# RWKV-7 and neighbourhood-attention trunk on one core: the inputs of the second and third stream of products are split one stream earlier

## The chip, the core and the metric

One core of a Trainium2 chip runs the whole program in one launch. The metric is the device time of one execution in microseconds (us). TensorE (PE) multiplies matrices, VectorE (DVE) and ScalarE (ACT) work on elements, GpSimd (POOL) sets small tiles and issues part of the stores, and SyncE (SP) issues the other DMAs. PSUM holds the results of products.

## What is computed

Two request groups of 512 tokens by 1024 features go through two layers with shared weights. Layer 0 is RWKV-7 time mixing, scanned forward and backward; layer 1 is 2-D neighbourhood attention. Everything is fp32.

```python
xx = 0.5 * (x_prev + x_next) - xn
lerp = lambda j: xn + xx * mu[j]
r = heads(lerp(0) @ w_r).astype(f32)
k = heads(lerp(1) @ w_k).astype(f32)
v = heads(lerp(2) @ w_v).astype(f32)
z = xn @ w_z
kk = k * k_k.astype(f32).reshape(N_HEADS, HEAD_DIM)
kk = kk / jnp.maximum(jnp.sqrt(jnp.sum(kk * kk, axis=-1, keepdims=True)), 1e-12)
...
for d in range(2):
    ...
    ys.append(_wkv7_scan(r, decay, k_d, v, -kk, kk * a, reverse=(d == 1)))
```

Layer 0 ends with a group norm per head, a gate by z and the product with `w_o`; layer 1 multiplies by `w_in` (1024 x 4096), attends within a window and multiplies by its own output weights.

## The kernel before

Activations lie with features on the 128 partitions and the 512 tokens along them, so a matrix of 1024 features is 8 tiles, called k tiles here. A product of one column (128 output features) takes 8 k tiles. fp32 operands are cut into a high and a low half (`halves`: ACT copies the rounded high half, DVE subtracts it), and a k tile costs three matmuls: high by high, high by low, low by high (L454 to L456 in `gemm`, L887 to L889 in the later stage). A column is therefore 24 matmuls. Its weights come as two raw tiles of 128x512 which are cut in the same way into `whi` and `wlo`, of which there are four buffers each (`NW`). Input halves lie in 18 buffers named `act`.

The program has four stages.

- **The head.** `prelude(0)` loads and normalises the first request group (its 1/rms comes from two small products, L482 and L496, in `rstd`), makes the low-rank products (L595 to L597; their weights lie in 16 buffers `lw`) and mixes neighbouring tokens for v (`mixed`, tiles `ls`, four buffers, stored to scratch DRAM). `prelude(1)` does the same for the second group, and mixes k, r and v for it. Both are generators; `run` takes one step of them for each k tile of PE's columns. PE's columns are first z (8 columns, products in PSUM tiles `zy`), then k (8 columns). The z columns read the unnormalised input (`xz`, 16 of the 18 `act` buffers).
- **Between them** `shifted(0, 1)` mixes k's inputs of the first group (a "lerp": ACT scales, DVE adds, tile `xr`) and cuts them into `act` halves. After the k columns `shifted(0, 0)` does the same for r.
- **The scan stage** (`scan_phase`). A planner (`weave`) interleaves threads by an estimate of when each engine is free, and the order that it finds is fixed for PE, DVE and ACT. `flow` runs the stream of 84 columns (r, v, then the second group's k, low-rank and z, r, v, then the first group's `w_o`, the rest of z, and 24 columns of `w_in`). `preps` makes the scan's factors of a pair of heads, `inverse` and `merges` invert small triangular matrices (DVE's elimination, L1096 and L1098, begins with a transpose at L1089), and `step` runs 64 scan steps, 8 for each of 8 pairs (L1298 is the product that solves a step). Where the planner foresees PE idle for over 0.3 us after a slack stretch it puts in a matmul without use (L1729, "filler"), which the hardware runs as two passes. The tiles of this stage (`k`, `r`, `rb`, `ab`, `cab`) lie where the head's `xn`, `xx`, `ls` and `lw` were, so they wait for these to be read.
- **The rest** is attention and the output products.

In a k column, `column` copies the product (L717), stores it, squares it (L726), sums the squares by head on PE (L730, a product of 2x512), copies the sums (L733) and stores them. After the last column the sums are read back, the square root and reciprocal taken (L744 to L747), stored as `rn`, and read as `rb` by the first `prep` (L962).

Engines take their instructions in order. So do the DMA issuers: an instruction that waits on SP holds up every transfer behind it.

Of the kernel before, what the change touches and what calls it, by code (L numbers as in the profile page):

```python
# [19 lines left out]
P = 128  # L20
T = 512
# [232 lines left out]
class Trunk:  # L254
# [274 lines left out]
    def prelude(self, s):  # L529
        nc = self.nc  # L530
        vt, gps, act = nc.vector, nc.gpsimd, nc.scalar
        xs = []
        if s == 0:
            self.vectors()
        for k in range(KT):
            if s == 0 and k == self.WFIRST:
                self.first = [self.weight(self.a["w_z"][0])]
            t = self.t("xn", (P, T + 2), 16, F32, self.lp)
            self.load(t[:, 1:T + 1], self.a["x"][s][k * P:(k + 1) * P, :])
            xs.append(t)  # L540
# [34 lines left out]
        def mixed(kind, j, k):  # L575

            t = self.t("ls", (P, T), 4, F32, self.lp)
            self.lerp(t, xn[k], xx[k], 8 * j + k)
            self.save("l" + kind, s, k, t)

        if s:
            for k in range(KT):
                for kind, j in (("k", 1), ("r", 0), ("v", 2)):
                    mixed(kind, j, k)
                    yield
                self.save("lz", s, k, xn[k])
            return
        pm = self.p("pf", (P, 2, T))
        ps = (self.p("pm"), self.p("us"))
        for k in range(KT):  # L590
            hi, lo = self.xz[k]
            for q2 in range(2):
                for out, w in ((pm[:, q2], self.wm), (ps[q2], self.wl)):
                    a, b = (m[:, k % 4] for m in w[2 * q2 + k // 4])
                    nc.tensor.matmul(out, a, hi, start=(k == 0), stop=False)  # L595
                    nc.tensor.matmul(out, a, lo, start=False, stop=False)
                    nc.tensor.matmul(out, b, hi, start=False, stop=(k == KT - 1))  # L597
                yield
        for q2 in range(2):
            mw = self.t("lm", (P, T + 2), 1, F32, self.lp)  # L600
            lr = self.t("lr", (P, KT * P), 1, F32, self.lp)
            y, u = lr[:, 0:T], lr[0:64, T:2 * T]
            gps.memset(mw[:, 0:1], 0.0)
            gps.memset(mw[:, T + 1:T + 2], 0.0)
            vt.tensor_tensor(mw[:, 1:T + 1], pm[:, q2], rstd, op=ALU.mult)
            vt.tensor_tensor(y, mw[:, 2:T + 2], mw[:, 0:T], op=ALU.add)
            yield
            vt.scalar_tensor_tensor(mw[:, 1:T + 1], y, 0.5, mw[:, 1:T + 1], op0=ALU.mult, op1=ALU.subtract)
            vt.tensor_tensor(y, ps[q2], rstd, op=ALU.mult)
            vt.tensor_tensor(y, y, mw[:, 1:T + 1], op=ALU.add)  # L610
            for q in (2 * q2, 2 * q2 + 1):
                act.activation(u, y[64 * (q % 2):64 * (q % 2) + 64], AF.Tanh if q < 2 else AF.Copy)
                self.hidden(q, u)
            yield
        for k in range(KT):
            mixed("v", 2, k)
            yield

    def lowrank(self, s, q2, shift, ps):
# [50 lines left out]
        self.nc.scalar.copy(h[0:64], u)  # L670
        self.nc.vector.tensor_tensor(h[64:128], u, h[0:64].bitcast(F32), op=ALU.subtract)

    def lerp(self, t, x, u, i):

        self.nc.scalar.activation(t, x, AF.Identity, scale=self.dv[:, 112 + i:113 + i])
        self.nc.vector.scalar_tensor_tensor(t, u, self.dv[:, 88 + i:89 + i], t, op0=ALU.mult, op1=ALU.add)

    def shifted(self, s, j):
# [93 lines left out]
        self.made.add((kind, s, p))  # L772

    def columns(self, s, kind, x, ps=range(NP)):
        for p in ps:
            w = self.first.pop() if self.first else self.weight(self.a["w_" + kind][p])
            ps = yield from self.gemm(w, x, self.gt)
            for _ in self.column(s, kind, p, ps):
                pass
            yield  # L780

    def flow(self):
# [7 lines left out]
        self.xq, self.post = x, {}  # L790
        for k, t in enumerate(self.groups[0][1]):
            x[0, k] = t

        def loads():
            for c, (_, _, src, _) in enumerate(cols):
                for j in range(2):
                    yield "S", lambda: did["load"] < did["split"] + self.NRAW
                    raw[2 * c + j] = t = self.t("raw", (P, self.WP), self.NRAW)
                    src(t, j) if callable(src) else self.load(t, src[:, j * self.WP:(j + 1) * self.WP])
                    did["load"] += 1  # L800

        def splits():
            for h in range(2 * len(cols)):
# [940 lines left out]
    def scan_phase(self, mid):  # L1744
# [69 lines left out]
        threads = [  # L1814
            Thread(lambda: 0, each(self.step)), Thread(lambda: 0.5, each(self.alone)), Thread(lambda: 0.5, each(self.near)),
            Thread(lambda: 1, each(self.outer)),
            Thread(lambda: 0, fetch()), Thread(lambda: 0, fetch_x()), *self.flow(), Thread(lambda: 5, inverse()), Thread(lambda: 2.4, merges()), Thread(lambda: 1.5, preps()),
            Thread(lambda: 1.3 if did["finish"] == 3 else 4, finish()), Thread(lambda: 1.2, self.norm0(0))]
        e = mybir.EngineType
        with self.tc.manual_schedule(engines={e.PE, e.DVE, e.Activation}):  # L1820
# [3 lines left out]
    def run(self):  # L1824
        self.todo = [(s, pb) for s in range(2) for pb in range(4)]
        self.made, self.hid, self.shift = set(), {}, {}
        self.did = Counter()
        self.xz, self.os = [], [[], []]
        self.spare = None
# [192 lines left out]
```

## Time and profile before

| | before |
|---|---|
| median of 3 runs | 1634.75 us (1633.54 to 1637.68) |
| profiled execution, its own time | 1627.3 us |
| its span from first to last instruction | 1625.5 us |
| PE busy | 1533.3 us, 94% of the span |
| DVE busy | 1218.4 us, 75% |
| ACT busy | 983.7 us, 61% |
| mean granted PE clock | 0.981 |

The profile lists for each engine how long it was busy, for each instruction when it began and what ended the idle time ahead of it, and the clock that PE was granted in a stretch (1.00 is full). Busy times of neighbouring matmuls overlap: a 128x512 matmul shows 0.39 us, but the next begins 0.23 us after it. Of the spans of the stages: the head up to the end of the z columns is 0 to 79.7 us, the k columns and what follows them up to the first r product 79.7 to 153.7, the scan stage 153.7 to about 1137, the rest up to 1625.5.

### The profile page before, as it was taken

The numbers are of one execution on the slowest core, as the hardware profiler recorded it, in microseconds if no ns is written. First come the engines' busy times: TensorE is split into PE (matmuls) and PEld (weight loads), VectorE is DVE, ScalarE is ACT, GpSimd is POOL, SyncE is SP. The second block draws the span as 40 slices with busy tenths as digits, with TensorE's granted clock in tenths as the row PEclk, the third lists the DMA queues.
The fourth block names the chain that finished last, engine by engine and source line by source line (L and its number), as shares of the span: only waits on it lengthen the run. The fifth ranks groups of instructions, "written<-read, shape, count | busy, mean of one in ns | idle before, by whom it ended". The sixth has DMA issues, their size and how long they took to land.

```text
span 1625.5 us, 46341 instructions
## 1 busy us (share of the span) xinstructions
PE 1533.3 (94%) x18748; PEld 1178.7 (73%) x18748; DVE 1218.4 (75%) x2714; ACT 983.7 (61%) x1949; POOL 179.2 (11%) x336
## 2 busy tenths in 40 slices
PE   7989999899989998988999999999999999999998
PEld 6866776666667676766677777777777788777776
DVE  8986587689778787876899998656676575754664
ACT  6567565757648456675666655544667665555562
POOL 0001124201011012231000011000000002100000
PEclk9989999999899999999999999999999999999999
DMA  6447687867576777677776775567664256645553
GB/s 242 158 169 260 212 279 237 270 195 245 167 251 227 239 248 218 224 242 242 247 262 212 233 262 180 160 191 245 196 226 155 93 162 223 224 165 185 163 162 104
DMA packets 182006, 340.46 MB, mean 209 GB/s; under 512 B 25344, under 2 KB 58240, under 8 KB 181792
## 3 DMA queue, kind: packets, MB, share of 16 engines
q1 hardware_dynamic: 158144, 256.75, 49.5%
q0 software_dynamic: 23648, 80.76, 13.9%
q8 instruction: 147, 2.41, 0.6%
q14 instruction: 67, 0.55, 0.1%
HBM read 230.33 MB, written 107.09 MB: 208 GB/s over the span
## 4 chain that ended last, share of the span: by engine, by line
PE 70%; DVE 11%; DMA 7%; issue 5%; ACT 5%; SPq 1%; DVEq 0%; POOL 0%; ACTq 0%; POOLq 0%
PE pm L887 8%; PE pg L454 7%; PE pg L455 6%; PE pg L456 6%; PE pm L888 6%; PE pm L889 6%; PE pf L1199 3%; DMA dab<-ab 2%; PE sc L1537 2%; PE po L1570 2%; PE us L1318 2%; PE pt L1555 2%; PE zy L1271 2%; PE us L1298 2%; DVE ab L1021 1%
## 5 line engine op out<-in xcount | busy, mean ns | idle before, releaser
L887 PE MATMUL pm<-act,whi 128*128 128x512 f32 x672 | 294.6, 438 | 2.7 <-ACT act L832 1.0
L888 PE MATMUL pm<-act,whi 128*128 128x512 f32 x672 | 268.0, 399 | 7.7 <-DVE act L834 6.8
L889 PE MATMUL pm<-act,wlo 128*128 128x512 f32 x672 | 267.3, 398 | 6.6 <-DVE wlo L808 6.6
L887 PEld LDWEIGHTS pm<-act,whi 128*128 128x128 f32 x672 | 127.7, 190 | 45.3 <-issue 12.2
L454 PE MATMUL pg<-act,whi 128*128 128x512 f32 x384 | 160.3, 418 | 0.0
L889 PEld LDWEIGHTS pm<-act,wlo 128*128 128x128 f32 x672 | 128.1, 191 | 37.2 <-DVE wlo L808 8.5
L888 PEld LDWEIGHTS pm<-act,whi 128*128 128x128 f32 x672 | 128.4, 191 | 33.9 <-DVE act L834 11.8
L455 PE MATMUL pg<-act,whi 128*128 128x512 f32 x384 | 152.8, 398 | 0.0
L456 PE MATMUL pg<-act,wlo 128*128 128x512 f32 x384 | 152.3, 397 | 0.0
L404 DVE TENSOR_TENSOR wlo<-raw,whi 128x512 fp32r<-128x512 f32 x148 | 101.6, 689 | 56.1 <-ACT whi L403 55.7
L403 ACT CAST whi<-raw 128x512 fp32r<-128x512 f32 x148 | 91.7, 619 | 83.0 <-PE pg L455 64.9
L808 DVE TENSOR_TENSOR wlo<-raw,whi 128x512 fp32r<-128x512 f32 x168 | 114.6, 684 | 29.1 <-ACT whi L806 29.1
L806 ACT CAST whi<-raw 128x512 fp32r<-128x512 f32 x168 | 103.8, 621 | 45.7 <-PE pm L888 39.5
L456 PEld LDWEIGHTS pg<-act,wlo 128*128 128x128 f32 x384 | 72.2, 188 | 14.9 <-issue 0.3
L454 PEld LDWEIGHTS pg<-act,whi 128*128 128x128 f32 x384 | 72.3, 188 | 14.4 <-issue 3.3
L1098 DVE TENSOR_TENSOR N<-etmp,N 128x30 f32<-128x30 f32 (+14 forms) x240 | 78.9, 329 | 4.6
L455 PEld LDWEIGHTS pg<-act,whi 128*128 128x128 f32 x384 | 72.5, 189 | 13.5 <-issue 2.8
L1096 DVE TENSOR_TENSOR etmp<-N 128x30 f32<-128x30 f32 (+14 forms) x240 | 78.8, 328 | 4.6
L1199 PE MATMUL pf<-cab 64*64 64x128 f32 (+1 forms) x2048 | 68.5, 268 | 6.3 <-issue 5.9
L1551 ACT ACTIVATE sb<-sb,mx 128x256 f32<-128x256 f32 x128 | 64.5, 506 | 11.4 <-DVE mx L1550 10.4
L1548 DVE CUSTOM_DVE_ANT_0 sb<-sc,bias 128x256 f32<-128x256 f32 x128 | 50.1, 420 | 24.3 <-PE pt L1555 13.3
L1310 ACT COPY X<-us 64x256 f32<-64x256 f32 x128 | 47.1, 368 | 33.5 <-PE zy L1177 31.7
(391 smaller groups left out, 3531.3 us busy)
## 6 DMA issues: line engine op xcount, KB each, us to landing
dab<-ab POOLq DMA_DIRECT2D x32, 1024.0 KB, 7.4
cab<-dab SPq DMA_DIRECT2D x64, 512.0 KB
raw<-in_w_in_dram SPq DMA_DIRECT2D x128, 256.0 KB
bias<-in_rpb_dram SPq DMA_DIRECT2D x32, 384.0 KB
raw<-in_w_z_dram SPq DMA_DIRECT2D x32, 256.0 KB
raw<-in_w_k_dram SPq DMA_DIRECT2D x32, 256.0 KB
raw<-in_w_r_dram SPq DMA_DIRECT2D x32, 256.0 KB
k<-dk SPq DMA_DIRECT2D x32, 256.0 KB
```

What stands on the lines that cost most here:

```text
L403: self.nc.scalar.copy(hi, src)
L404: (eng or self.nc.vector).tensor_tensor(lo, src, hi.bitcast(F32), op=ALU.subtract)
L454: nc.tensor.matmul(ps, hi, x[k][0], start=(k == 0), stop=False)
L455: nc.tensor.matmul(ps, hi, x[k][1], start=False, stop=False)
L456: self.mm = nc.tensor.matmul(ps, lo, x[k][0], start=False, stop=(k == KT - 1))
L806: nc.scalar.copy(hi, raw[h])
L808: nc.vector.tensor_tensor(lo, raw.pop(h), hi.bitcast(F32), op=ALU.subtract)
L887: nc.tensor.matmul(ps, hi[:, at], xh, start=(k == 0), stop=False)
L888: nc.tensor.matmul(ps, hi[:, at], xl, start=False, stop=False)
L889: nc.tensor.matmul(ps, lo[:, at], xh, start=False, stop=(k == KT - 1))
L1098: vt.tensor_tensor(N[:, q + 1:, :q], tv, N[:, q + 1:, :q], op=ALU.add)
L1199: end = nc.tensor.matmul(st.f[half(a), h, 0, d, g] if st.last else st.f[half(a), h, :, d, g], ab[half(h), d, g, 2 * e[d] + 1 - a], rt if s ...
```

## The change

The k inputs of the first group are mixed and cut within `prelude(0)`, in the place of the v mixes, and their halves go into the `lw` buffers, which the low-rank products have left. The v mixes move to the start of `prelude(1)`'s mixes, right behind its normalisation, and so into the k columns; each waits (`past`) for the matmul of `gemm` that was written last ahead of it. `prelude(1)` waits 14 steps (`HOLD`) ahead of its 1/rms. A new generator `ahead` runs beside the k columns, one step for every four k tiles (`RATE`): it mixes and cuts the r inputs into `act`, and loads and cuts the first r column's two weight halves, which hold two of the four weight buffers until the scan stage. In `columns` a k column's head sums (product, copy, store) are issued four k tiles into the next column; those of the last column become a thread of the scan stage (`tail`), with a gate at 2.5 us of the planner's time.

```diff
+    RATE, HOLD = 0.25, 14
...
+        for _ in range(s * self.HOLD):
+            yield
         rstd = self.rstd(acc, (lambda: self.mm) if s else None)
...
         if s:
             for k in range(KT):
+                self.mixed(0, "v", 2, k, self.mm)
+                yield
+            for k in range(KT):
                 for kind, j in (("k", 1), ("r", 0), ("v", 2)):
-                    mixed(kind, j, k)
+                    self.mixed(s, kind, j, k)
                     yield
...
+        for k in range(KT):
+            hi, lo = (self.t("lw", (P, 4, 2, 64), 16, F32R, self.lp).rearrange("p k q c -> p (k q c)") for _ in range(2))
+            t = self.t("xr", bufs=self.NXR)
+            self.lerp(t, xn[k], xx[k], 8 + k)
+            self.xk.append(self.halves(t, lo, hi))
+            yield
...
+    def ahead(self):
+        xn, xx = self.shift[0]
         for k in range(KT):
-            mixed("v", 2, k)
+            lo, hi = self.pair()
+            t = self.t("xr", bufs=self.NXR)
+            self.lerp(t, xn[k], xx[k], k)
+            self.xr.append(self.halves(t, hi, lo))
+            yield
+        for raw in self.raws(self.a["w_r"][0]):
+            hi, lo = (self.t(tag, (P, self.WP), self.NW, F32R) for tag in ("whi", "wlo"))
+            self.wr.append(self.halves(raw, lo, hi))
             yield
...
+    def lerp(self, t, x, u, i, past=None):
+        one = self.nc.scalar.activation(t, x, AF.Identity, scale=self.dv[:, 112 + i:113 + i])
+        if past is not None:
+            self.after(one, [past])
...
     def columns(self, s, kind, x, ps=range(NP)):
+        self.tail = None
         for p in ps:
...
+                n += 1
+                if n == 4 and self.tail:
+                    run(self.tail[1])
+                    self.tail = None
+                yield
+            end = self.column(s, kind, p, out)
+            if kind == "k":
+                for _ in range(3):
+                    at = next(end)
+                self.tail = at, end
+            else:
+                run(end)
             yield
...
+        w.update(enumerate(self.wr))
+        did["load"] = did["split"] = len(w)
...
+        def tail():
+            (eng, gate, needs), end = self.tail
+            yield eng, gate, lambda c: max(needs(c), 2500.0)
+            yield from end
...
-        run(self.columns(0, "k", self.shifted(0, 1)), (a, 1))
+        run(self.columns(0, "k", self.xk), (a, 1), (self.ahead(), self.RATE))
         run(a)
-        self.xr = self.shifted(0, 0)
```

The order of instructions shows it at three places. Line numbers of the changed kernel differ: L455 to L457 are its `gemm`, L483 and L497 the two small products of the 1/rms, L756 the head sums, L934 to L936 the products of the stream, L699 the lerp's ACT part, L743 and L759 the copies of a column and of its sums.

On PE, the first k column stood around the 1/rms of the second group (`pm_865`, `pm_878`) before; here are the rows where its fifth k tile (`act_943`) begins.

```order
L455 MATMUL zy_979<-act_935,whi_971 128x512
L456 MATMUL zy_979<-act_936,wlo_972 128x512
L454 MATMUL zy_979<-act_943,whi_975 128x512
L482 MATMUL pm_865<-ones,acc_782 128x1 x4
L455 MATMUL zy_979<-act_942,whi_975 128x512
L456 MATMUL zy_979<-act_943,wlo_976 128x512
L454 MATMUL zy_979<-act_950,whi_975 128x512
```

Now the same products stand between the third and the fourth k column (`zy_1061`, `zy_1138`), with two head sums (`pm_1006` of the first, `pm_1079` of the second column) beside them.

```order
L457 MATMUL zy_1061<-lw_706,wlo_1058 128x512
L483 MATMUL pm_976<-ones,acc_798 128x1 x4
L497 MATMUL pm_989<-tmp_984,ones 128x128
L756 MATMUL pm_1006<-tmp_951,cc 2x512
L497 MATMUL pm_989<-tmp_984,ones 128x128 x3
L756 MATMUL pm_1079<-tmp_1039,cc 2x512
L455 MATMUL zy_1138<-lw_616,whi_1130 128x512
```

The 1/rms moved two and a half columns back, and no column's matmul stands between its four steps any longer.

On PE, between the last k column (`zy_1471`) and the first r column (`pm_1618`), before:

```order
L455 MATMUL zy_1471<-act_963,whi_1467 128x512
L456 MATMUL zy_1471<-act_964,wlo_1468 128x512
L730 MATMUL pm_1454<-tmp_1452,cc 2x512
L730 MATMUL pm_1502<-tmp_1500,cc 2x512
L1729 MATMUL zy_1594<-cc 128x256 x6
L887 MATMUL pm_1618<-act_1518,whi_1609 128x512
L888 MATMUL pm_1618<-act_1517,whi_1609 128x512
```

And now (`zy_1527` is the last k column, `pm_1601` the first r column, whose inputs `act` and weights `whi_1279` are there already):

```order
L456 MATMUL zy_1527<-lw_707,whi_1523 128x512
L457 MATMUL zy_1527<-lw_706,wlo_1524 128x512
L756 MATMUL pm_1547<-tmp_1508,cc 2x512
L934 MATMUL pm_1601<-act_928,whi_1279 128x512
L935 MATMUL pm_1601<-act_929,whi_1279 128x512
```

The six fillers are gone from this place, one of the two head sums is left, and the last column's sums follow 12 matmuls into the r column.

On ACT, the start of the scan stage before: the last two of r's halves, then the square root (L744) and the first weights of the stream.

```order
L675 ACTIVATE xr_1563<-xn_137,dv 128x512
L403 CAST act_1560<-xr_1556 128x512
L1756 COPY cab_418_1582<-cc 64x64 x2
L1756 COPY cab_419_1583<-cc 64x64 x2
L403 CAST act_1567<-xr_1563 128x512
L744 ACT_TABLE_LOAD
L744 ACTIVATE tmp_1507<-tmp_1507 128x64
L832 CAST act_1616<-xr_1599 128x512
L806 CAST whi_1628<-raw_1607 128x512
```

And now, where the last mixes of the second group (`ls`) stand among the stream's weights (`whi`) and ahead of the copies into `cab` and of the first `prep` (L1011):

```order
L770 ACTIVATE tmp_1648<-tmp_1648 128x64
L853 CAST whi_1714<-raw_1667 128x512
L699 ACTIVATE ls_1486<-xn_794,dv 128x512
L699 ACTIVATE ls_1496<-xn_796,dv 128x512
L743 COPY tmp_1717<-pm_1651 128x512
L699 ACTIVATE ls_1510<-xn_796,dv 128x512
L699 ACTIVATE ls_1531<-xn_796,dv 128x512
L1803 COPY cab_420_1582<-cc 64x64 x2
L1803 COPY cab_421_1583<-cc 64x64 x2
L1011 CAST w2h_1695<-tmp_1696 128x512
L853 CAST whi_1747<-raw_1699 128x512
```

The square root has no table load of its own now, and four mixes, all of which stood in the k columns, stand behind it.

More of the change, by code (lines that the diff above doesn't have):

```diff
@@ L573, in prelude @@
         self.shift[s] = xn, xx
[L575 to L579, printed above, removed]
         if s:
             for k in range(KT):
+                self.mixed(0, "v", 2, k, self.mm)
+                yield
+            for k in range(KT):
                 for kind, j in (("k", 1), ("r", 0), ("v", 2)):
-                    mixed(kind, j, k)
+                    self.mixed(s, kind, j, k)
                     yield
@@ L614, in prelude, with mixed @@
             yield
-        for k in range(KT):
-            mixed("v", 2, k)
+    def mixed(self, s, kind, j, k, past=None):
+        xn, xx = self.shift[s]
+        t = self.t("ls", (P, T), 4, F32, self.lp)
+        self.lerp(t, xn[k], xx[k], 8 * j + k, past)
+        self.save("l" + kind, s, k, t)
+    def ahead(self):
+        xn, xx = self.shift[0]
+        for k in range(KT):
+            lo, hi = self.pair()
[6 more added lines that the diff above has]
+            self.wr.append(self.halves(raw, lo, hi))
             yield
@@ L671, in hidden @@
         self.nc.vector.tensor_tensor(h[64:128], u, h[0:64].bitcast(F32), op=ALU.subtract)
-    def lerp(self, t, x, u, i):
-        self.nc.scalar.activation(t, x, AF.Identity, scale=self.dv[:, 112 + i:113 + i])
+    def lerp(self, t, x, u, i, past=None):
+        one = self.nc.scalar.activation(t, x, AF.Identity, scale=self.dv[:, 112 + i:113 + i])
+        if past is not None:
+            self.after(one, [past])
         self.nc.vector.scalar_tensor_tensor(t, u, self.dv[:, 88 + i:89 + i], t, op0=ALU.mult, op1=ALU.add)
@@ L774, in columns @@
     def columns(self, s, kind, x, ps=range(NP)):
+        self.tail = None
         for p in ps:
             w = self.first.pop() if self.first else self.weight(self.a["w_" + kind][p])
-            ps = yield from self.gemm(w, x, self.gt)
-            for _ in self.column(s, kind, p, ps):
-                pass
+            gemm, n = self.gemm(w, x, self.gt), 0
+            while True:
+                try:
+                    next(gemm)
+                except StopIteration as end:
+                    out = end.value
+                    break
+                n += 1
[10 more added lines that the diff above has]
+                run(end)
             yield
@@ L796, in loads @@
                 for j in range(2):
+                    if 2 * c + j < len(self.wr):
+                        continue
                     yield "S", lambda: did["load"] < did["split"] + self.NRAW
@@ L802, in splits @@
         def splits():
-            for h in range(2 * len(cols)):
+            for h in range(len(self.wr), 2 * len(cols)):
                 yield "A", lambda: h < did["load"] and h < did["k"] // 4 + self.NW, lambda c: c.at(name(raw[h]))
@@ L1816, in scan_phase @@
             Thread(lambda: 1, each(self.outer)),
-            Thread(lambda: 0, fetch()), Thread(lambda: 0, fetch_x()), *self.flow(), Thread(lambda: 5, inverse()), Thread(lambda: 2.4, merges()), Thread(lambda: 1.5, preps()),
+            Thread(lambda: 0, tail()), Thread(lambda: 0, fetch()), Thread(lambda: 0, fetch_x()), *self.flow(), Thread(lambda: 5, inverse()), Thread(lambda: 2.4, merges()), Thread(lambda: 1.5, preps()),
             Thread(lambda: 1.3 if did["finish"] == 3 else 4, finish()), Thread(lambda: 1.2, self.norm0(0))]
@@ L1828, in run @@
         self.xz, self.os = [], [[], []]
+        self.xk, self.xr, self.wr = [], [], []
         self.spare = None
```

## Prediction

> **What bounds the kernel now.** I read the busy time by stage first, then PE's timeline at the two places where a stream of inputs gives way to the next, then what the scan stage waits for. Columns: the stretch, its length, busy us of PE, PEld, DVE, ACT and POOL with instruction counts, granted PE clock, DMA share, GB/s.
>
> ```profile
> 79.70:153.70 74.00, 63.88 (x237) 44.28 (x236) 59.87 (x97) 57.48 (x100) 3.67 (x3) 0.88 0.60 209
> 305.00:993.00 688.00, 639.55 (x11343) 483.12 (x11341) 583.60 (x1140) 429.68 (x821) 95.34 (x159) 0.98 0.72 234
> 993.00:1137.00 144.00, 141.32 (x2728) 108.78 (x2729) 94.45 (x199) 70.84 (x138) 8.70 (x15) 1.00 0.59 192
> ```
>
> In the 74 us of the k columns PE is idle for 10 us, runs at a clock of 0.88 and does fillers besides. In the scan stage PE and DVE are both busy (93% and 85% up to 993 us); from 993 to 1137 us PE alone is full. PE's timeline around the k columns (start, length, instruction, in brackets the idle time ahead and what ended it):
>
> ```profile
> 78.31 0.39 PE L454 MATMUL zy<-act,whi 128*128 128x512 f32 x1
> 78.53 0.39 PE L455 MATMUL zy<-act,whi 128*128 128x512 f32 x1
> ...
> 83.55 0.50 PE L454 MATMUL zy<-act,whi 128*128 128x512 f32 x1 [1.00 <-ACT act L403]
> 87.11 1.84 PE L482 MATMUL pm<-ones,acc 128*128 128x1 f32 x8 [3.06 <-DVE acc L469]
> ...
> 89.39 0.63 PE L456 MATMUL zy<-act,wlo 128*128 128x512 f32 x1
> 89.81 0.63 PE L454 MATMUL zy<-act,whi 128*128 128x512 f32 x1
> ...
> 95.02 0.39 PE L455 MATMUL zy<-act,whi 128*128 128x512 f32 x1
> ...
> 103.21 1.02 PE L730 MATMUL pm<-tmp,cc 128*2 128x512 f32 x2 [2.32 <-ACT tmp L726]
> ...
> 135.97 0.39 PE L456 MATMUL zy<-act,wlo 128*128 128x512 f32 x1
> ...
> 137.23 0.50 PE L454 MATMUL zy<-act,whi 128*128 128x512 f32 x1
> ...
> 147.65 1.87 PE L730 MATMUL pm<-tmp,cc 128*2 128x512 f32 x2 [3.73 <-ACT tmp L726]
> 149.45 4.61 PE L1729 MATMUL zy<-cc 128*128 128x256 f32 x12
> 153.71 0.59 PE L887 MATMUL pm<-act,whi 128*128 128x512 f32 x1
> ```
>
> The reader is to see four losses. The k inputs are late (1.00 us), the 1/rms of the second group holds the column (3.06), and after this idle time a matmul follows the last after 0.43 us instead of 0.23 until 95. Then 2.32 and 3.73 us for squares that ACT has not made, and a tail of sums and fillers, 149.45 to 153.71, in which r's inputs are finished. A row of the kind 135.97 to 137.23 shows the price of a head sum within a column: 1.26 us to the next matmul instead of 0.23, so 1.03 us.
>
> **The change, step by step.** All times are of the profiled execution (1627.3 us, 7.45 below the median shown; I add the change to the median).
>
> The prices of the pieces (line, operation, count, then busy us and mean ns of one, then idle time ahead):
>
> ```profile
> L676 DVE SCALAR_TENSOR_TENSOR xr<-xx,dv,xr 128x512 f32<-128x512 f32 x12 | 8.9, 750 | 1.6 <-ACT xr L675 1.6
> L404 DVE TENSOR_TENSOR act<-xr,act 128x512 fp32r<-128x512 f32 x13 | 8.8, 690 | 2.1 <-ACT act L403 2.1
> L675 ACT ACTIVATE xr<-xn,dv 128x512 f32<-128x512 f32 x12 | 8.3, 717 | 1.8 <-DVE act L404 1.8
> L403 ACT CAST act<-xr 128x512 fp32r<-128x512 f32 x12 | 7.2, 609 | 1.1 <-DVE xr L676 1.1
> L726 ACT ACTIVATE tmp<-zy,cv 128x512 f32<-128x512 f32 x8 | 5.4, 680 | 0.0
> L717 ACT COPY tmp<-zy 128x512 f32<-128x512 f32 x8 | 4.6, 571 | 1.8 <-PE zy L456 1.8
> ```
>
> Where does the first r product come? The z columns are unchanged and end at 79.7. DVE stands almost without idle time there, so the new work must fit: eight k inputs cost it a lerp (0.75) and a cut (0.69) each, while eight v lerps leave and the 1/rms and five normalisations (0.75 each) move behind; 11.5 us come and about 10 go. By DVE's order, summed with these durations, the last k half is made at about 64 us and the weights of the third k column at about 88, some 5 us ahead of PE. I cost this at nothing; its cover is that lead. Then: 192 matmuls at 0.227 are 43.5 us; seven head sums 7 x 1.03 = 7.2; the two products of the 1/rms 1.8, between which PE now has no column to do. That stall I add up from these rows of ACT and DVE:
>
> ```profile
> 88.34 1.28 ACT L487 ACT_TABLE_LOAD   x1
> 89.64 0.27 ACT L487 ACTIVATE rs<-pm,eps 128x4 f32<-128x4 f32 x1
> 89.80 0.62 ACT L612 ACTIVATE lr<-lr 64x512 f32<-64x512 f32 x1
> 93.89 0.62 ACT L670 CAST h<-lr 64x512 fp32r<-64x512 f32 x1
> ```
>
> The third k column ends at 96.0 (79.7 + 16.3). ACT casts the last weights that it frees (0.6), loads its table (1.28), takes the root (0.27); then four instructions for the low-rank part, which took 4.7 us here (89.80 to 94.51) and wait for DVE half way, I take 3.4; a copy and the second column's copy and square, 1.8. So the second head sum starts at 103.4 and the fourth column at 104.4: 8.4 us, of which 3.8 are sums and 1/rms, so 4.6 of stall. The sixth column has a head sum after two matmuls (0.45 us), and copy and square (0.57 and 0.68) with PE's own end before them take about 1.5: 1.0 more. Total 79.7 + 43.5 + 7.2 + 1.8 + 4.6 + 1.0 = 137.8, against 153.71: the r products start 15.9 us earlier. The r inputs cost DVE 8 x (0.75 + 0.69) = 11.5 us beside the k columns; DVE's 59.9 us in this stage, in the first row above, nearly fill the 58 us that are left of it, so what gives way is the work that comes last in DVE's order, the mixes, not the halves. Two of four weight buffers are held by the first r column: a half can then be cut only when the half before it in use is done, 2.7 us ahead of need, against 1.3 us of cutting; nothing, with 1.4 us of cover.
>
> The clock is the open price here. In the rows above it fell to 0.69 and 0.50 for the 3.06 us gap, but not for the 2.32:
>
> ```profile
> 84.00:86.00 2.00, 0.05 (x1) 0.00 (x0) 2.00 (x4) 1.17 (x2) 0.00 (x0) 0.69 0.02 6
> 86.00:88.00 2.00, 0.89 (x5) 0.92 (x5) 2.00 (x4) 0.40 (x1) 0.00 (x0) 0.50 0.52 158
> 100.00:102.00 2.00, 0.89 (x4) 0.39 (x3) 2.00 (x5) 2.00 (x5) 0.00 (x0) 1.00 0.99 380
> ```
>
> The new stall lies in two pieces of about 2.0 and 2.3 us with small products between. I take no fall, and 3 us for the range (some 7 us at half clock, as from 88 to 95).
>
> The Trainium skill (TensorE: Matmul & The Clock Gate, Part 1) puts the fall after at least one idle window of about 3.4 us. By it neither piece of the new stall can cost clock and r starts at 137.8; by the row, where the clock fell 0.7 us into a gap after 1.00 us of earlier waiting, two close gaps may, and r starts at 140.8. The trace disagrees with the rule as worded, and so the 3 us stay in the range.
>
> When can the scan begin? Its first `prep` waits for `rb`, and for the head's tiles to be read.
>
> ```profile
> L676 DVE SCALAR_TENSOR_TENSOR ls<-xx,dv,ls x24: 743/752/758, 110.5 to 144.6; 128x512 f32<-128x512 f32 x24
> 116.00:125.00 9.00, 9.00 (x38) 6.51 (x37) 5.45 (x8) 7.01 (x12) 0.00 (x0) 1.00 0.91 310
> 159.69 1.15 SPq L356 DMA_DIRECT2D rb<-drn  x2
> 163.49 0.75 DVE L962 SCALAR_TENSOR_TENSOR rb<-k,cv,rb 128x512 f32<-128x512 f32 x1 [2.08 <-DMA rb<-drn]
> ```
>
> Before: the last head sum ends at 149.5 and L962 starts at 163.49, 14.0 us later. Now the last sum ends at 137.8 + 2.7 + 1.0 = 141.5, which would give 155.5. But 32 mixes instead of 24 must go through four `ls` buffers, each with a store, and `rb` is issued on SP behind the last store; the later v loads (`xr`) wait on SP for their own stores just ahead of weights. The mixes before took 34.8 us (110.5 to 145.3), 1.45 each, with the DMAs at 0.91. They now start at about 111.7 (normalisation from 104, eight at 0.67, four sums at 0.6). At 1.45 the last ends at 158.1, and `prep` starts 4.3 later, 162.4; at DVE's bare 0.75 they are out of the way. The added wait on PE's matmuls (columns four and five) costs nothing, since DVE's order brings the mixes no sooner. I take 157, nearer to the sum's chain, as ACT's order leaves four mixes behind the first r column's copy: 6.5 us earlier than 163.5. Both ends, 8 and 1, stay for the range. So of the 15.9 us on PE about 9 meet a scan that is not ready.
>
> What is that worth later?
>
> ```profile
> L1089 DVE STREAM_TRANSPOSE N<-Gd x8: 1902/1970/2096, 224.3 to 984.3; 128x1024 f32<-128x1024 f32 x8
> 153.70:305.00 151.30, 12.75 (x46) 8.73 (x44) 0.98 0.74 239
> 305.00:993.00 688.00, 19.18 (x68) 13.96 (x68) 0.98 0.72 234
> ```
>
> The first row is the transpose that opens each elimination: seven intervals of 109 us from 224 to 984, though the stream's next columns are there, so PE has slack (the other two rows are fillers alone, 31.9 us). The stage goes by the chain prep, elimination, merge, 8 steps. Between the first and the last of these transposes DVE's rows, each with its line's mean duration, sum to 591.7 us before and 588.5 now: the chain has the same work. So it keeps its 6.5 us. From 993 PE is full, and when the 50th step begins 72 columns have begun in both orders, so the lead goes through to the end. Sum: 1627.3 - 6.5 = 1620.8; on the median 1634.75 - 6.5 = 1628.2.
>
> **The rivals.** *All of PE's lead arrives.* If PE's work is what sets the end, the 15.9 us count: 1618.9. For it: PE is full from 993. Against: the fillers and 109 us intervals above.
>
> *The lead is lost in the scan.* The planner's order holds 62 fillers before, six of them ahead of the first r product, and 89 now: 33 more after it. At 31.9 us for 57 pairs of passes, 0.56 each, that is 18.5 us; at the bare spacing of two passes, 0.44, 14.5. Taken as idle time in the PE sum, 15.9 less 14.5 to 18.5: 1633 to 1637. Against it: fillers stand where PE would wait anyway.
>
> *Slower.* The last group of the stream (24 columns) needs eight inputs that DVE and ACT make; before, beside steps 41 to 47:
>
> ```profile
> L842 DVE SCALAR_TENSOR_TENSOR xr<-xr,cv,acc x6: 705/746/772, 856.3 to 904.3; 128x512 f32<-128x512 f32 x6
> L858 DVE SCALAR_TENSOR_TENSOR act<-xr,cv,act x6: 743/748/750, 884.3 to 906.9; 128x512 fp32r<-128x512 f32 x6
> L867 ACT ACTIVATE tmp<-xr x5: 621/632/642, 888.6 to 906.9; 128x512 f32<-128x512 f32 x5
> ```
>
> Its first product stood after 44 begun steps and now stands after 49, in a gap without steps, with 20 fillers within its first column. An input costs four DVE passes (0.75, 0.69, 0.75, 0.69) and two of ACT (0.72, 0.63), 4.2 us in a row; four of them uncovered are 17 us, 1628.2 + 17 = 1645. It decides from 11.5 us uncovered on.
>
> **How the numbers follow.** Likeliest, 0.42: the chain's lead, 1628, with its own 1623 to 1633. All of PE's lead: 0.16. Lost in the scan: 0.25. Slower: 0.17. A measurement of this kernel can tell about 0.3%, 4.9 us, from no change. The likeliest lies 1.6 us past that bound, so I count a quarter of it as no change: faster 0.32 + 0.16 = 0.48, same 0.10 + 0.25 = 0.35, slower 0.17. The range goes from 1616 (PE's whole lead and a little) to 1641, which leaves out the larger half of the slower case.
>
> **What would show it.** Right: r's first product at 138 to 141; a PE gap of 4 to 5 us between the third and fourth k column; the first `prep` at 155 to 160; the first transpose at 216 to 220, the last at 976 to 980. Wrong: k columns that wait for halves or weights (DVE without lead); mixes past 160; transposes that spread to more than 109 us; the last group's first column long after its neighbours.

## The result, and the profile after

The changed kernel is slower: 1649.1 us median (1641.7 to 1657.3, 14 runs) against 1633.9 (14 runs), a ratio of 1.0094 with a 95% interval of 1.0071 to 1.0117. The forecast was 1628, with 1616 to 1641 as its range. The profiled executions took 1647.8 us (span 1646.0) and 1627.3 (span 1625.5), so the two traces differ by 20.5 us and the medians by 15.2. Differences read within the two traces below add up to the first of these numbers.

The part of the change that the diff describes does what it says. PE at the two places of the prediction, in the changed kernel (start, length, instruction, idle time ahead and what ended it):

```profile
79.76 0.39 PE L455 MATMUL zy<-lw,whi 128*128 128x512 f32 x1
...
96.33 0.39 PE L457 MATMUL zy<-lw,wlo 128*128 128x512 f32 x1
96.56 0.95 PE L483 MATMUL pm<-ones,acc 128*128 128x1 f32 x8
99.44 0.46 PE L497 MATMUL pm<-tmp,ones 128*128 128x128 f32 x2 [1.94 <-DVE tmp L493]
...
104.49 0.50 PE L455 MATMUL zy<-lw,whi 128*128 128x512 f32 x1
...
161.18 0.72 PE L934 MATMUL pm<-act,whi 128*128 128x512 f32 x1 [2.84 <-ACT whi L853]
161.69 0.63 PE L935 MATMUL pm<-act,whi 128*128 128x512 f32 x1
167.41 0.79 PE L936 MATMUL pm<-act,wlo 128*128 128x512 f32 x1 [5.08 <-DVE wlo L855]
```

The k columns follow the z columns without a gap, and the first r product starts at 140.5 us instead of 153.7. The reader is to see that the lead is already being lost at 158 to 167, in two waits of 2.84 and 5.08 us for the halves of an r weight. The second is a matter of DVE's order: the missing half is cut right behind the first instruction of the first `prep` (L1009, at 166.00), which itself had waited for a DMA.

```profile
166.66 0.69 DVE L855 TENSOR_TENSOR wlo<-raw,whi 128x512 fp32r<-128x512 f32 x1
```

Between the first r product and the last product of the stream the window of before reads (columns as in the prediction's windows):

```profile
153.70:1137.00 983.30, 919.49 (x15467) 699.64 (x15466) 782.63 (x1523) 594.34 (x1137) 143.01 (x236) 0.98 0.70 229
```

and that of after:

```profile
140.50:1158.50 1018.00, 942.60 (x15541) 718.44 (x15541) 795.78 (x1538) 602.18 (x1154) 146.29 (x239) 0.97 0.69 225
```

The stream and the scan take 34.7 us longer: 13.2 of them eat the lead, and the other 21.5 are the loss. PE is 23 us busier (fillers, and a lower clock), and idle for 75 us instead of 64. The transposes that open the eight eliminations come late at the first (231.5 against 224.3, 7.2 us), stand within 5 us of before at the second and third (314.9 and 414.4 against 316.3 and 409.5) and are 14.6 us behind at the last, 998.9 against 984.3:

```profile
L1136 DVE STREAM_TRANSPOSE N<-Gd x8: 1954/1980/2074, 231.5 to 998.9; 128x1024 f32<-128x1024 f32 x8
```

One place stands out to the eye. The stream's last group begins with column 60 (columns are counted from 0), whose inputs are made just ahead of it. From its first product to that of column 61 pass 27.3 us, 16.6 before. The window over just this stretch, of after:

```profile
915.00:942.40 27.40, 22.64 (x213) 16.66 (x211) 26.86 (x45) 16.14 (x31) 2.46 (x4) 0.94 0.73 248
```

and of before, where more matmuls lie in fewer us, 321 against 213:

```profile
894.70:911.30 16.60, 14.84 (x321) 11.36 (x319) 15.54 (x29) 11.13 (x21) 0.12 (x1) 1.00 0.66 215
```

PE's timeline of after shows the stretch, 40 passes of fillers (L1776) and waits for inputs that ACT and DVE are still making:

```profile
918.30 0.39 PE L936 MATMUL pm<-act,wlo 128*128 128x512 f32 x1
921.37 3.72 PE L1776 MATMUL zy<-cc 128*128 128x256 f32 x16
927.21 0.49 PE L934 MATMUL pm<-act,whi 128*128 128x512 f32 x1 [2.12 <-ACT act L903]
...
928.82 5.30 PE L1776 MATMUL zy<-cc 128*128 128x256 f32 x16
934.82 1.03 PE L1776 MATMUL zy<-cc 128*128 128x256 f32 x4
...
936.51 0.50 PE L935 MATMUL pm<-act,whi 128*128 128x512 f32 x1 [0.44 <-DVE act L905]
...
937.08 1.02 PE L1776 MATMUL zy<-cc 128*128 128x256 f32 x4
```

It does not show where the time went, though. Columns 60, 61 and 62 start at 894.7, 911.3 and 928.6 us before and at 915.1, 942.4 and 950.5 after. So column 60 already begins 20.4 us late; column 61 takes 8.1 us instead of 17.3 and gives nearly all back; and column 62 begins 21.9 us late, as the last column does (21.8). The order also moves scan products from one column to another: in after, column 48 begins 31 us sooner than before and column 56 begins 21 us later. The length of one column is therefore no measure of a loss.

### The profile page after: what moved, and what is told of

It reads as the page before. It is cut to its first block, busy times and chain, and to the rows that moved or that the text cites. A ratio compares the mean times of both kernels' runs of the same rounds, so it can differ in the third digit from the quotient of the medians.

```text
span 1646.0 us, 46466 instructions
## 1 busy us (share of the span) xinstructions
PE 1548.4 (94%) x18802; PEld 1192.0 (72%) x18802; DVE 1221.4 (74%) x2714; ACT 978.3 (59%) x1945; POOL 178.7 (11%) x336
## 4 chain that ended last, share of the span: by engine, by line
PE 67%; DVE 12%; DMA 7%; ACT 7%; issue 6%; SPq 0%; POOL 0%; DVEq 0%; ACTq 0%; POOLq 0%
PE pm L934 7%; PE pg L455 6%; PE pg L456 6%; PE pg L457 6%; PE pm L936 5%; PE pm L935 5%; PE pf L1246 2%; PE sc L1584 2%; PE po L1617 2%; DMA dab<-ab 2%; PE pt L1602 2%; PE zy L1318 2%; PE us L1365 2%; PE us L1345 2%; PE zy L1369 1%
## 5 line engine op out<-in xcount | busy, mean ns | idle before, releaser
L934 PE MATMUL pm<-act,whi 128*128 128x512 f32 x672 | 296.1, 441 | 7.9 <-ACT whi L853 2.8
L935 PE MATMUL pm<-act,whi 128*128 128x512 f32 x672 | 268.3, 399 | 13.2 <-DVE act L881 11.2
L936 PE MATMUL pm<-act,wlo 128*128 128x512 f32 x672 | 267.3, 398 | 5.1 <-DVE wlo L855 5.1
L934 PEld LDWEIGHTS pm<-act,whi 128*128 128x128 f32 x672 | 127.9, 190 | 53.6 <-issue 16.3
L455 PE MATMUL pg<-act,whi 128*128 128x512 f32 x384 | 160.4, 418 | 0.0
L936 PEld LDWEIGHTS pm<-act,wlo 128*128 128x128 f32 x672 | 128.2, 191 | 34.4 <-DVE wlo L855 5.8
L457 PE MATMUL pg<-act,wlo 128*128 128x512 f32 x384 | 152.3, 397 | 0.0
L457 PEld LDWEIGHTS pg<-act,wlo 128*128 128x128 f32 x384 | 72.2, 188 | 15.1 <-issue 0.3
L455 PEld LDWEIGHTS pg<-act,whi 128*128 128x128 f32 x384 | 72.3, 188 | 14.4 <-issue 3.3
L1269 DVE TENSOR_TENSOR AK<-zy,cc 128x256 f32<-128x256 f32 x63 | 26.6, 423 | 51.4 <-PE zy L1224 50.4
```

Source lines behind the costliest of these rows:

```text
L455: nc.tensor.matmul(ps, hi, x[k][0], start=(k == 0), stop=False)
L457: self.mm = nc.tensor.matmul(ps, lo, x[k][0], start=False, stop=(k == KT - 1))
L934: nc.tensor.matmul(ps, hi[:, at], xh, start=(k == 0), stop=False)
L935: nc.tensor.matmul(ps, hi[:, at], xl, start=False, stop=False)
L936: nc.tensor.matmul(ps, lo[:, at], xh, start=False, stop=(k == KT - 1))
```

## The experiments

Two theories were put against each other. *Order*: the time is lost because the planner, which writes the order of the scan stage while the kernel is built, began from another state (one r column's weights cut already, a k sum still to come) and drew a longer order. *Start*: it is lost in the changed start itself, by the late mixes, the late r weights and the clock. Every ratio below is to the kernel before, run on the same chip in the same rounds.

### Two starts, two orders

The planner's choices were listed and repeated in the other kernel, with the choices that only one of them has left out or added:

```diff
+    ORDER = (
+        "jtk......jkokohkoojoohioiopopthoioioooo
...
         while True:
-            ts = [t for t in threads if not t.over]
...
+            late = next(t for t in threads if t.gen.__name__ == "tail")
+            if late.open() and late.ready(ck) <= now + self.EPS:
+                best = late
+            else:
+                best = row.pop(0)
```

Each letter is a thread, a dot is a filler.

> The changed kernel, but the scan stage is written in the order that the planner drew for the kernel before (its 4125 decisions are listed in the kernel and repeated; the two loads and four cuts of the first r column, which the change does earlier, are left out of the list, and the last k column's sum goes in where the first 2.5 us of the plan are over). Theory 'order' (the 15 us are lost because the planner, from another starting state, drew a longer order for the scan): near the kernel before or faster, 1622 to 1637 us, with the last product of the stream at 1125 to 1140 instead of 1158. Theory 'start' (the 15 us come from the changed start itself: 8 more mixes late, the r weights behind their stores, a cooler clock, prep 2.5 us later): it stays at 1645 to 1652.

> The kernel before, but the scan stage is written in the order that the planner drew for the changed kernel (4151 decisions, with the loads and cuts of the first r column put ahead and the last k column's sum left out). Theory 'order': 1645 to 1660 us, as slow as the changed kernel or slower, since it has not even the earlier first r product. Theory 'start': 1630 to 1638, as the kernel before.

The changed kernel in the order of before: 1636.4 us, ratio 1.0015 (0.9992 to 1.0038), the same time as before. The kernel before in the order of after: 1648.2 us, ratio 1.0086 (1.0057 to 1.0115), as slow as the changed kernel. So the order carries the loss and the start does not; theory "start" is refuted by both. One number of the first expectation was missed (1125 to 1140): the stream's last product stood at 1151.2 us in the profiled execution, which at 1641.9 was the slowest of its kernel.

The first of the two had a flaw. The order of before has six fillers (12 passes) ahead of the first r product, and the last k sum came ahead of it too, so the first r product came at 151.3 us and the lead was not tried. A third kernel kept it:

```diff
-        "jtk......jkokohkoojoohioiopopthoioioooo
+        "jtkjkokohkoojoohioiopopthoioioooo
...
-            if late.open() and late.ready(ck) <= now + self.EPS:
+            if did["k"] >= 4 + did["tail"] and late.open():
+                did["tail"] += 1
```

> As the run of the changed kernel with the order of the kernel before, but its PE lead is kept: the six fillers ahead of the first r product are left out of the order, and the last k column's sum stands behind the first four of r's inputs instead of ahead of them. The first r product should come at 140 to 143 instead of 151. What is 10 us of PE worth, with one order? Theory 'prep' (the scan goes from the start of its first prep, which stays at 164 to 169 as its sums, its k and rb come through busy DMA queues): 1632 to 1638 us. Theory 'PE lead': 1636 - 10 = 1626 or less, 1620 to 1628.

Measured: 1633.7 us, ratio 0.9981 (0.9961 to 1.0000). Its first r product stands at 141.5, 12.2 us ahead of the kernel before. Its transposes:

```profile
L1163 DVE STREAM_TRANSPOSE N<-Gd x8: 1892/1974/2106, 223.2 to 986.9; 128x1024 f32<-128x1024 f32 x8
```

Its window from the first r product to the stream's last:

```profile
141.50:1140.00 998.50, 922.73 (x15467) 700.40 (x15467) 793.74 (x1537) 603.53 (x1156) 146.36 (x239) 0.97 0.70 229
```

In one and the same order 12.2 us of lead on PE become 12.0 us more of idle time (998.5 - 922.7 = 75.8, against 983.3 - 919.5 = 63.8). Of these 12 us, 10.2 stand in three waits before 180 us: 3.3 and 5.8 for `w2h` and `w2l`, the halves of a weight that the first `prep` cuts, and 1.1 for a weight half; the kernel before waits 0.2 us between 150 and 180. The transposes go from 223.2 to 986.9, within 3 us of before. The lead itself is worth 0 to 6 us by the interval, and theory "PE lead" is refuted (1620 to 1628 expected). The number of theory "prep" came (`prep` at 165.0), but that the time follows the first `prep` is not shown. In the five kernels that share the order of before, up to its first choices (the two controls below among them), `prep` starts at 160.3, 163.5, 165.0, 167.0 and 170.6, and the ratios are 0.9983, 1, 0.9981, 1.0001 and 1.0015: over 10.3 us of `prep` the time moves by about 0.3%, some 5 us, which is hardly beyond the intervals.

### Other orders from the same starts

Is an order that is 15 us longer something special? EPS says by how many ns the planner may take an instruction before it is ready; another value gives another order and changes nothing else.

```diff
-    NZ1, STOCK, EPS, NEAR = 4, 1, 60.0, 400.0
+    NZ1, STOCK, EPS, NEAR = 4, 1, 90.0, 400.0
```

> The changed kernel with one number of the planner changed: EPS, by how many ns an instruction may be taken before it is ready, 90 instead of 60. Nothing is added or removed but fillers (43 planned instead of 89). By the planner's own account the scan then takes 972.4 us instead of 993.5 (977.7 for the kernel before). Theory 'order': about 1649 - 21 = 1628, between 1620 and 1636. Theory 'start': 1645 to 1652, since the start is the same.

> The kernel before with EPS 70 instead of 60: by the planner's own account the scan takes 1000.2 us instead of 977.7. Theory 'order', in the form that any redrawn plan may be some 10 to 20 us longer whatever the change to the start: 1634 + 22 = 1656, between 1646 and 1662. Theory 'start': 1630 to 1640, as the kernel before.

The planner's account and the chip, side by side (the account is the planner's own clock at its last choice; it is no measurement):

| kernel | planner's account, us | planned fillers | median, us | ratio (95%) |
|---|---|---|---|---|
| changed, EPS 90 | 972.4 | 43 | 1632.7 | 0.9981 (0.9957 to 1.0005) |
| before, EPS 60 | 977.7 | 62 | 1633.9 | 1 |
| changed, EPS 60 | 993.5 | 89 | 1649.1 | 1.0094 (1.0071 to 1.0117) |
| before, EPS 70 | 1000.2 | 78 | 1665.0 | 1.0183 (1.0146 to 1.0220) |

The chip follows the account in its order (the first two are the same within the interval) and about in size: 16.4 us between the two orders of the changed kernel (21.1 by the account), 31.1 between those of before (22.5; the 1665.0 lie 3 us above what was expected). The kernel before can be made 31 us slower by one number, and the changed one 16 us faster.

The account can be read at many values of EPS. With 43 values from 30 to 100 (the even ones and the multiples of five) the kernel before gave 975.4 to 1002.9, mean 985.7, and four values were better than its 60. At the same 43 values the changed kernel gave 972.4 to 998.9, mean 986.9, and 34 were better than its 60. Changed less before goes from -21.9 to +18.9 with a mean of +1.2. These are accounts of built orders; four of these orders ran on the chip. They speak for a redraw: the change moved the kernel from one of the best orders of its start to one of the slowest fifth of the other, and does not make orders longer in general.

Where within the order the time goes stays open. Column 60 lasted 16.6 to 17.0 us in the eight profiles with the order of before or of EPS 90 (those below that share these orders included), 27.0 to 27.5 in the five with the order of after, and 35.1 with EPS 70 in the kernel before. But columns 60 and 61 together took 32.7 to 34.4 us in the eight and 33.5 to 35.4 in the five, so the length of column 60 alone does not price the order; with EPS 70 the two took 48.1. Nor do the eliminations tell the end. With EPS 90 the last transpose comes still later than in the changed kernel, 18.6 us behind the kernel before, and the median is as before:

```profile
L1136 DVE STREAM_TRANSPOSE N<-Gd x8: 1936/1977/1993, 230.2 to 1002.9; 128x1024 f32<-128x1024 f32 x8
```

### The fillers

> The changed kernel in its own order, with all 89 planned fillers (178 passes, 124 in the kernel before) left out and nothing else moved. Theory 'fillers' (the 54 passes more cost the time, 0.22 to 0.28 us each, 12 to 15 us, and the others besides): 1610 to 1637 us. Theory 'order' (the fillers stand in waits that the order makes, and fill them): 1644 to 1654 us, with idle time on PE where they stood, and more of it at half clock.

The dots are taken out of the listed order of after; the first of them:

```diff
-...thototooitt.hii.itotototohiiqotq...
+...thototooitthiiitotototohiiqotq...
```

Measured: 1658.6 us, ratio 1.0149 (1.0114 to 1.0184), 9.5 us slower than the changed kernel. Theory "fillers" is refuted; "order" was right about the sign and 5 us short of the time. From 170 to 1000 us, without fillers:

```profile
170.00:1000.00 830.00, 743.93 (x12244) 559.26 (x12243) 671.42 (x1290) 503.97 (x968) 129.10 (x214) 0.93 0.71 230
```

and in the changed kernel, with them:

```profile
170.00:1000.00 830.00, 766.42 (x12489) 583.46 (x12489) 674.40 (x1292) 505.38 (x970) 129.75 (x216) 0.96 0.70 231
```

The clock falls from 0.96 to 0.93 without them. So fillers stand in waits and keep the clock up here; 89 instead of 62 is a sign of a longer order, not its price.

### What holds the first prep

In the changed kernel the last of 32 mixes is made at 159.9, and the first prep starts 2.5 us later than before, though PE is 13 us ahead. The mixes of after, then the timelines of SP and DVE around the first prep, and then the load of `k` before:

```profile
L702 DVE SCALAR_TENSOR_TENSOR ls<-xx,dv,ls x32: 741/751/754, 111.7 to 159.1; 128x512 f32<-128x512 f32 x32
```

```profile
153.20 1.00 SPq L357 DMA_DIRECT2D drn<-tmp  x1
159.88 0.32 SPq L351 DMA_DIRECT2D dlv<-ls  x1
160.38 1.15 SPq L357 DMA_DIRECT2D rb<-drn  x2
161.57 0.58 SPq L357 DMA_DIRECT2D k<-dk  x1
166.00 0.75 DVE L1009 SCALAR_TENSOR_TENSOR rb<-k,cv,rb 128x512 f32<-128x512 f32 x1 [4.18 <-DMA k<-dk]
```

```profile
151.92 0.38 SPq L356 DMA_DIRECT2D k<-dk  x1
```

The sums' result is on its way at 153.2, but `rb` is loaded at 160.4 and `k` at 161.6, behind the last mix's store. Two edits, each with a control in the kernel before:

```diff
-        t = self.t("ls", (P, T), 4, F32, self.lp)
+        t = self.t("ls", (P, T), 5, F32, self.lp)
```

```diff
-        self.save("l" + kind, s, k, t)
+        self.sp["l" + kind, s, k] = d = self.dram(f"l{kind}{s}{k}", t.shape)
+        self.nc.gpsimd.dma_start(d, t)
```

> The changed kernel with five ls buffers for the mixes instead of four; the order of the scan stage is the same, decision for decision. In the trace of the changed kernel the 32 mixes take 1.50 us each (111.7 to 159.9) and ACT and DVE wait 9.0 us for their stores; prep starts at 166.0. Theory 'mixes' (the stores of four buffers set the pace, and so the start of prep and the late r weights): 1.2 us a mix, the last before 154, prep at 157 to 161, and this lead goes through the scan: 1640 to 1644 us. Rival 'DMA' (the DMAs, 0.8 to 0.96 busy there, set the pace): prep at 164 to 167, 1646 to 1652. Rival 'lost later': prep earlier by 5 and more, but the time 1646 to 1652.

> The kernel before with five ls buffers, the control for the two others. There the last mix was made at 145.3 and prep started at 163.5, 14 us after the last head sum, so by every theory the buffers are not its limit: 1630 to 1637 us.

> The changed kernel, same order decision for decision, with the 32 mixes stored through POOL's queue instead of SP's. In the trace of the changed kernel the store of drn is issued on SP at 153.2, but rb, which reads it, stands behind the last two mixes' stores and is issued at 160.4; k follows at 161.6 and prep starts at 166.0. Theory 'queue' (SP's order holds prep): rb at 155 to 158, prep at 160 to 163, the time 1643 to 1646. Rival 'DMA' (the transfers themselves are late, the DMAs being 0.87 busy from 120 to 165): prep at 164 or later, 1647 to 1652.

> The kernel before with its 24 + 8 mixes stored through POOL's queue: the control. There rb was issued at 159.7, 3.6 us after drn's store and with nothing else ahead of it on SP for 2.1 us, so it waits for drn itself: 1630 to 1637 us by every theory, prep at 162 to 165.

None moved the time: 1649.2 (ratio 1.0081, 1.0049 to 1.0114) with five buffers, 1648.7 (1.0076, 1.0044 to 1.0109) with POOL's queue, and the controls 1630.1 (0.9983, 0.9960 to 1.0006) and 1634.3 (1.0001, 0.9975 to 1.0027). In the changed kernel prep started at 167.6 in both, so "mixes" (1640 to 1644 expected) and "queue" (1643 to 1646) are refuted; "DMA" had the times right, and with five buffers its prep (164 to 167) was 0.6 us short. In the controls prep started at 160.3 and 167.0; the second missed its 162 to 165. The same rows with five buffers:

```profile
L702 DVE SCALAR_TENSOR_TENSOR ls<-xx,dv,ls x32: 737/745/754, 111.7 to 155.4; 128x512 f32<-128x512 f32 x32
```

```profile
155.56 0.45 SPq L357 DMA_DIRECT2D drn<-tmp  x1
157.18 0.63 SPq L351 DMA_DIRECT2D dlv<-ls  x1
161.34 1.16 SPq L357 DMA_DIRECT2D rb<-drn  x2
167.62 0.75 DVE L1009 SCALAR_TENSOR_TENSOR rb<-k,cv,rb 128x512 f32<-128x512 f32 x1 [11.18 <-DMA k<-dk]
```

With POOL's queue, the timeline of SP and that of ACT:

```profile
151.97 0.33 SPq L357 DMA_DIRECT2D drn<-tmp  x1
...
161.23 1.15 SPq L357 DMA_DIRECT2D rb<-drn  x2
```

```profile
159.84 1.33 ACT L700 ACTIVATE ls<-xn,dv 128x512 f32<-128x512 f32 x2 [0.49 <-DMA dlk<-ls]
```

Five buffers end the mixes 3.7 us sooner, as "mixes" said; then the store of `drn` takes 5.7 us to land instead of 3.0, and `k` 5. With POOL's queue nothing stands ahead of `rb` on SP for 7.7 us, and still it is issued at 161.2, when ACT's last mix ends (159.84 + 1.33 = 161.17). The built program of this run says why: this load waits for the landing of `drn`, for a count on POOL and for a count on ACT that ACT's last mix completes, and `rb` is given memory of two of the tiles `xn` that the last mixes read. So one wait stands behind the other: SP's order, the stores' landing, the last mix.

> The changed kernel with EPS 90 (its shorter order, 1632.7 us on the chip) and five ls buffers together. Theory 'mixes': 1632.7 less 5 to 9, 1624 to 1628. Rivals 'DMA' and 'lost later': 1630 to 1636.

> The changed kernel with EPS 90, five ls buffers and the mixes' stores on POOL's queue: the shorter order with both holders of prep removed. Theory 'queue': prep at 158 to 162 and 1632.7 less 4 to 8, 1625 to 1629. Rival 'DMA': 1631 to 1636.

In the order of EPS 90 five buffers alone gave 1632.7 us, ratio 0.9997 (0.9973 to 1.0020): nothing. With POOL's queue besides, 1630.5 us, ratio 0.9955 (0.9931 to 0.9980), with prep at 163.8 instead of 168.0 in the profiles. Its time lies between the two expectations (1625 to 1629 for "queue", 1631 to 1636 for "DMA") and decides for neither. This is the only kernel that is faster than before clear of its interval, by 0.45%; it is 1.1% faster than the changed kernel by the medians and 1.4% by the ratios, and most of that is the order. Its own gain over EPS 90 alone, 0.9955 against 0.9981, lies within the intervals.

## Why the prediction was wrong

**The first r product** (137.8 forecast, 140.5 measured) was right to 2.7 us, just inside the 138 to 141 that it gave. The stretch of the 1/rms came out in the sum, in part by luck: third k column's end to the fourth's start 8.4 us forecast, 104.49 - 96.56 = 7.9 measured, though only 2.2 us of it were plain idle time instead of 4.6, and the rest was slow matmuls, since the clock fell. Of what is missing, 1.2 us are 192 matmuls at 0.233 instead of 0.227.

**The first prep** (157 forecast, 155 to 160 named as right, 162.4 as the late end) was wrong: 166.0. The pace of the mixes was sized well, 48.2 us / 32 = 1.50 each against 1.45, and the last ended at 159.9 instead of 158.1. The failed step is the choice of 157 between ends that it had itself worked out, and the 4.3 us behind the last mix, which were 6.2: `k`, loaded at 151.9 in the kernel before, now came behind `rb`. The cover of the weight halves, put at nothing because only the mixes would give way, failed with it: PE waited 2.84 and 5.08 us for them. The first transpose, expected at 216 to 220, came at 231.5.

**"So it keeps its 6.5 us"** is the step that failed and cost the range. It took equal sums of DVE work between the transposes (591.7 and 588.5 us) for equal time, and so put the redrawn order at nothing. The work was equal: in the traces DVE is busy 637.4 and 633.9 us between the first and the last transpose. But in the order of after it took 767.4 us instead of 760.0, and the stream lost time besides; the runs with exchanged orders put 13 to 15 us on the order alone. The rest of the 21.7 us between the 6.5 us forecast as gain and the 15.2 measured as loss is the gain itself, which did not come in the order of before either (ratios 1.0015 and 0.9981). A sum of work says nothing of the waits in which it is ordered. That the chain of eliminations carries its lead or delay to the end is not borne out either: with EPS 90 the last transpose is 18.6 us behind before, at the same median.

**The rivals.** "Slower" had the right sign, and its total, 1645, was 4 us from the measured one; it had 0.17. That is luck in good part. The waits and the 20 fillers that it named in the last group's first column are there, and the column took 10.7 us more, against 17 forecast. But the column already began 20.4 us late, and with the next column the two took 1.5 us more. "Lost in the scan" had the loss of the lead right, and its price, a cost for each filler, wrong: without fillers the kernel is slower still. "All of PE's lead" is refuted by the run that kept the lead in the order of before. The argument against it, that fillers and idle time show slack on PE, was the right one for this lead, and 12.0 us of new idle time agree with it.

**The clock.** The stall was taken without a fall, and it had one, for about 3.4 us:

```profile
98.00:100.00 2.00, 0.56 (x3) 0.38 (x4) 1.09 (x6) 1.89 (x4) 0.00 (x0) 0.96 0.37 129
100.00:102.00 2.00, 2.00 (x3) 0.37 (x2) 0.66 (x2) 1.29 (x3) 0.00 (x0) 0.50 0.01 2
102.00:104.00 2.00, 1.73 (x8) 1.07 (x7) 0.69 (x2) 1.96 (x4) 0.00 (x0) 0.68 0.11 42
```

The Trainium skill (TensorE: Matmul & The Clock Gate, Part 1) has the clock fall after at least one idle window of about 3.4 us. Here it fell after 1.94 us without a matmul, with eight short ones of 128x1 just ahead; the trace disagrees with the rule as worded, as it did before.

What stays open: why the planner's choices from the two starts part as they do was not followed choice by choice, and where within the longer order its 13 to 15 us are lost is not shown.

## What to carry to other kernels

Where a planner writes the order, every edit ahead of it redraws the rest, and the redraw (16 to 31 us here, from one number) can be larger than the edit. Hold the order fixed, or tune its numbers anew on both sides, before an edit is judged; a kernel whose number was tuned is compared at one of its luckiest orders (only four of 43 values had a better account here). And a lead on a busy engine can be worth next to nothing if what it meets is not early too: here 12 us of lead turned into 12 us of idle time, 9.1 of them in waits for the first `prep`, which started no sooner than before (165.0 against 163.5).

## What the runs showed of the hardware

The 128x512 matmuls of k, whose moving tiles now lie in the `lw` buffers, follow each other after 0.2331 us (some 175 pairs between 79.8 and 139.0 us, at full clock), and the z columns' from `act` tiles after 0.2274 (some 135 pairs between 30 and 79); before, the k columns from `act` tiles took 0.2278. The difference, 2.5%, was not tried further.

The store of `drn`, 32 KB, landed after 3.0 us in the changed kernel and after 5.7 with five buffers, and DMA is 0.87 busy from 120 to 165 us in the first. Here freeing a buffer ended the mixes 3.7 us sooner and the first `prep` still started at 167.6 instead of 166.0.
